# Three modulation rows summed over the partitions by adding transfers instead of by ones-matmuls

## The chip, the cores and the metric

The kernel runs on one core of one Trainium2 chip. The metric is the device time of one execution in microseconds (us); the time before is the median of three runs. Beside them stands one profiled execution of the same kernel, from which all rows below are taken; its times are counted from the start of its span.

## The reference, cut to what matters

One layer of a diffusion backbone on 1024 latent tokens of width 1024 with 256 context tokens. What matters here is the modulation: six rows of 1024 numbers made of the condition `c`, of which three (the shift and scale ahead of the MLP, and the gate behind the mixing sub-layer) are worked out early and used late.

```python
mod_x = (jax.nn.silu(c) @ w_mod[l] + b_mod[l])[:, None, :]
sh1, sc1, gt1, sh2, sc2, gt2 = jnp.split(mod_x, N_MOD, axis=-1)
h_x = _modulate(x, g_pre_mix[l], sh1, sc1)
u_x, q_x, k_x, v_x = _project(h_x, w_in[l])
attn_x = _neighbourhood_attention(q_x, k_x, v_x, k_c, v_c, rpb[l])
mix_x = jnp.concatenate([_pool_mixer(u_x, ...), attn_x], axis=-1) @ w_out[l]
x = x + gt1 * _rmsnorm(mix_x, g_post_mix[l])
y_x = _sq_relu_mlp(_modulate(x, g_pre_mlp[l], sh2, sc2), w_mlp_in[l], w_mlp_out[l])
x = x + gt2 * _rmsnorm(y_x, g_post_mlp[l])
```

## The kernel before

The program is one long line of matmuls on TensorE (PE); the other engines prepare operands and carry results away. Around the change the line is: the key and query products (a Strassen-like scheme of seven products per side, `half_product`, in steps 0 to 23), then 32 attention units `i = (j, m)`, four head pairs `j` by eight token tiles `m`, about 3 us each. Two query products that are left over (`last_query`) fill PE in units 0 and 1. Within the stretch that interests here the order on every engine is the order in which the code is written (`in_order` ties each instruction to the one before it on its engine), so an instruction that waits holds up all that is written behind it on that engine. SyncE (SP) issues the plain transfers; transfers that add (`add_to`) are issued by GpSimd (POOL).

The three rows. `mod_begin` clears a page of 128 x 1024 in SBUF (`accsh`, `accsc`, `acca` for shift, scale and gate; the bias goes into row 0), and `mod_add` adds a 128-row block of the weight times a column of the condition on VectorE (DVE), eight times. Each page then holds 128 partial sums, which are still to be summed over the partitions. The shift's page is stored to DRAM at once (`kept_row`, `row` in the profile) and given back; the other two stay in SBUF.

In units 0 to 6 the sums are finished. `mod_sums_of` multiplies a page by a matrix of ones (four matmuls of 256 columns, so that quarter c of the row stands on partitions 32c to 32c+31); for the gate VectorE multiplies that by `gain`, the norm's gain `gp1` loaded by four broadcasting transfers; for scale and shift ScalarE (ACT) copies it back (`column_sums`). `mod_out` stores the four quarters to DRAM by four transfers of POOL for each row (`ga`, `gsc`, `gsh`). They are read again much later: `columns_of` at units 10 and 12, `gate_page` at unit 30.

What stands beside this work on POOL's queue: `tables(0)`, the bias tables `tab` of the first heads, made of `msk` and `U0w`; `query_parts` and `key_parts` (a cast and a difference each, `qP`, `kP2l`); four adding transfers `y<-y`; and in each unit the copy of the softmax's reciprocal sums, `rb<-ri` (`share`). PE's `turn(i)` in unit i + 2 begins with a transpose of `rb` (line 1312 `pa<-ident,rb`), then transposes the probabilities (`T<-ident,sp`); ACT takes them away (`fifth_kept`, `px`; `turn_kept`, `pt`) and goes on with the exponentials of the unit (`exps`, line 1290); `values` (line 1346) multiplies `pt` by the values. `scores` (line 1259) needs the split keys and queries (`kP0h`, `kP0l`, `qP`), and `biased` on VectorE (line 1279) needs the table.

Near the end of the kernel a fourth row, `accb`, is already summed in the other way: `rows_folded` adds the lower half of the rows to the upper half by one adding transfer, seven times (64, 32, ..., 1 rows). Its lines are

```python
def add_to(to, more):
    nc.gpsimd.dma_start(to, more, accum_op=add)

def rows_folded(rows, *counts):
    for n in counts:
        add_to(rows[:n], rows[n : 2 * n])
```

Of the kernel before, what the change touches and what calls it, by code (L numbers as in the profile page):

```python
# [11 lines left out]
F32 = mybir.dt.float32  # L12
# [6 lines left out]
P = 128  # L19
D = 1024  # L20
# [88 lines left out]
def hybrid_block(ctx, tc, x, ctx_in, w_mod, mod_pages, w_u, b_mod, gp1, gp2, w_in, pool_w, rpb, w_out, w1, w2, vectors,  # L109
                 mask, edge, out):  # L110
    nc = tc.nc
    sub, mul, add = ALU.subtract, ALU.mult, ALU.add
# [6 lines left out]
    dram = ctx.enter_context(tc.tile_pool(name="dram", bufs=1, space=DRAM))  # L119

    def cst(name, shape, dt=F32):
        return const.tile(shape, dt, tag=name, name=name)
# [4 lines left out]
    def page(name, dt=F32):  # L127
        return act.tile([P, 1024], dt, tag="pg", name=name)
# [23 lines left out]
    ones = cst("ones", [P, P])  # L152
# [65 lines left out]
# [3 lines that stand above are left out]
# [40 lines left out]
            mod_add(acc, mod_part(name, c, k), sT, k)  # L261
            yield acc


    def mod_sums_of(name, acc, bank):
        ps = bank(f"pg{name}")
        for c in range(4):
            nc.tensor.matmul(ps[32 * c : 32 * c + 32, :256], ones[:, :32], acc[:, c * 256 : (c + 1) * 256],
                             start=True, stop=True)
        return ps[:, :256]  # L270

    def mod_gain(gp, g, queue):
        quarters = gp.rearrange("(c o f) -> c o f", c=4, o=1)
        for c in range(4):
            queue.dma_start(g[32 * c : 32 * c + 32, :], quarters[c].to_broadcast([32, 256]))
        return g

    def mod_gate(name, acc, g, bank):
        nc.vector.tensor_tensor(acc[:, :256], mod_sums_of(name, acc, bank), g, mul)


    def mod_out(name, acc):
        gates[name] = dram.tile([1, D], F32, tag=f"g{name}", name=f"g{name}")
        for c in range(4):
            nc.gpsimd.dma_start(gates[name][:, c * 256 : (c + 1) * 256], acc[32 * c : 32 * c + 1, :256])

    gates = {}

# [14 lines left out]
    with tc.tile_pool(name="ps1", bufs=6, space=PSUM) as ps1, tc.tile_pool(name="tmp1", bufs=3) as tmp:  # L303

        def bank(name):
            if name[:2] == "pm" or name in ("pxt5", "pxb2", "pxb3", "pxb4", "pxb5", "pcs", "pcr"):
                return lasting(name)
            return ps1.tile([P, 512], F32, tag="mm", name=name)
# [526 lines left out]
        accs = {}  # L835


        kept_row = dram.tile([P, D], F32, tag="row", name="row")

        def mod_parts(name, c, n):  # L840
            accs[name] = mod_begin(name, c, page)
# [4 lines left out]
                    nc.gpsimd.dma_start(kept_row, accs[name])  # L846
                yield


        def column_sums(name, acc, bank):  # L850
            nc.scalar.copy(acc[:, :256], mod_sums_of(name, acc, bank))

        def columns_of(name, to):
            nc.gpsimd.dma_start(to, gates[name].rearrange("o (k p) -> p (o k)", p=P))
# [116 lines left out]
        with tc.issue_after(last[ET.DVE]), tc.issue_after(last[ET.Activation]):  # L971
            for i in range(2):
                ps = bank(f"pvc{i}")
# [49 lines left out]
        rows = [("sc", 4, k) for k in range(4, KT)] + [("a", 2, k) for k in range(KT)]  # L1023
# [22 lines left out]
        def use(step):  # L1046
            for _, put, i in islice(uses, len(plan[step + 1]) if step + 1 < len(plan) else 0):
                put(i)
                fetch()
# [9 lines left out]
        for n, m in enumerate((4, 5, 6, 7, 0, 1, 2, 3)):  # L1059
            ps = bank(f"pv{m}")  # L1060
# [123 lines left out]
        with in_order(ET.PE, ET.Pool, ET.Activation, ET.DVE, ET.SP) as pooling:  # L1184
            banks = {of: [bank(f"p{of}{j}") for j in range(2)] for of in "KQ"}
            use(-1)
            for step, (n, of, j) in enumerate([(n, of, j) for n, of in products for j in range(2)]):
                half_product(n, of, j, banks[of])
                use(step)
                if step in (5, 9, 17):  # L1190
                    name = {5: "S1", 9: "S4", 17: "S3"}[step]
                    parts = token_operand(name, sraw[name])
                if step in (5, 7, 9, 11, 17, 19):
                    next(parts)
                    next(parts)
                if step in (7, 11):
                    name = {7: "S4", 11: "S3"}[step]
                    sraw[name] = token_raw(name)
                if step == 14:
                    mask_page()  # L1200
                if step == 20:
                    for _ in tables(0):
                        pass
                if step in (21, 22):
                    for g in range(2):
                        pool_mixed(2 * (step - 21) + g)
                kept_product(n, of, j, banks[of][j])
                if step == 10:
                    kcs += [page(f"kc{n}", F32R) for n in "hl"]
                    split(kcp, *kcs)  # L1210
                if step == 22:
                    key_parts(0, 0, True)
# [17 lines left out]
    with (  # L1230
# [4 lines left out]
        bank = lasting  # L1235
# [3 lines left out]
        pa, pz = (ps_o.tile([P, 512], F32, tag=n, name=n) for n in ("pa", "pz"))  # L1239
# [208 lines left out]
        with in_order(ET.PE, ET.Activation, ET.DVE, ET.SP) as projected:  # L1448
# [16 lines left out]
            def right_added(j):  # L1465
# [2 lines left out]

            table = [None] + [tables(j) for j in (1, 2, 3)]
            built = lambda j: next(table[j])  # L1470
            out_of = lambda n: mod_out(n, accs[n])
            jobs = {0: [(built, 1), (key_parts, 1, 0), (key_parts, 1, 1)], 1: [(built, 1)], 2: [(built, 1)], 3: [(built, 1)],
                    4: [(built, 1)], 5: [(out_of, "a"), (out_of, "sc")], 6: [(out_of, "sh")], 7: [(query_parts, 1, 1, True, True)],
                    8: [(mixed_split, 0, True)], 9: [(built, 2)],
                    10: [(columns_of, "sc", scale2), (built, 2)], 12: [(columns_of, "sh", s2), (built, 2)],
                    13: [(built, 2), (built, 2)], 14: [(query_parts, 3, 0, False, True)],
# [2 lines left out]
                    21: [(built, 3), (built, 3)], 22: [(key_parts, 3, 1, False, True)], 24: [(mixed_split, 2, True)],  # L1479
                    25: [(query_parts, 3, 1, False, True)], 26: [(weight_split, 0, True)], 28: [(weight_split, 1, True)],  # L1480
                    29: [(weight_split, 2, True)], 30: [(weight_split, 3, True)]}
            rest_of_bank = lambda name: pz[:, 256:]
            for i in range(N):
                if i in LOADS:
                    weight_load(0, kks[LOADS.index(i)])
                if i == N - 2:
                    G1 = gate_page("a")
                if i > 3:
                    weighed(i - 4)
                if i == 0:  # L1490
                    gain = mod_gain(gp1, att.tile([P, 256], F32, tag="gp", name="gpa"), nc.sync)
                    accs["sh"] = page("accsh2")
                    nc.sync.dma_start(accs["sh"], kept_row)
                if i == 2:
                    mod_gate("a", accs["a"], gain, rest_of_bank)
                if i in (5, 6):
                    for k in (2 * i - 10, 2 * i - 9):
                        nc.sync.dma_start(sa2[k], s3[k])
                low()
                scores(i)  # L1500
                biased(i, 0)
                if i < N - 1:
                    biased(i, 1)
                if 8 < i and i % 8 == 3:
                    right_added(i // 8 - 1)
                if 8 < i and i % 8 == 7:
                    add_to(heads[i // 8 - 1][:, :512], sa2[i // 8 - 1])
                for f, *args in jobs.get(i, ()):
                    f(*args)
                if block_copies and (i < 4 or 6 < i):  # L1510
                    block_copied()
                for _ in range(SUMS.count(i)):
                    block_summed()
                if i == 2:
                    late_query = part_page("qP0_1", False)
                    qparts[0, 1] = late_query[:, :512], late_query[:, 512:]
                    high_part(qT[0][1], qparts[0, 1][0])
                if i > 1:
                    turn(i - 2)
                    fifth_kept(i - 2)  # L1520
                if i == 2:
                    turn_kept(0, 0, nc.scalar.copy)
                    column_sums("sc", accs["sc"], lambda name: pa[:, :256])
                if i == N - 1:
                    turn_kept(i - 2, 0, nc.scalar.copy)
                    turn_kept(i - 2, 1, nc.vector.tensor_copy)
                    biased(i, 1)
                exps(i, 0)
                if i == 2:
                    column_sums("sh", accs["sh"], rest_of_bank)  # L1530
                if 2 < i < N - 1:
                    turn_kept(i - 2, 0, nc.scalar.copy)
                exps(i, 1)
                if i == 0:
                    key_parts(2, 0, True, "lo")
                    key_parts(2, 1, True, "lo")
                    query_parts(2, 0, False, "lo")
                if 1 < i < N - 1:
                    turn_kept(i - 2, 1, nc.vector.tensor_copy)
                if i == 2:  # L1540
                    low_part(qT[0][1], *qparts[0, 1])
                for filler in fillers.get(i, ()):
                    last_query(*filler)
                if i > 2:
                    values(i - 3)
# [80 lines left out]
    with tc.tile_pool(name="ps2", bufs=6, space=PSUM) as ps2:  # L1626
# [6 lines left out]
      with ExitStack() as tmp2:  # L1633
# [28 lines left out]
        rows, root = {}, {}  # L1662
# [29 lines left out]
        with tc.issue_after(projected[ET.DVE]), tc.issue_after(projected[ET.Activation]), in_order(ET.Activation, ET.DVE, ET.Pool) as added:  # L1692
# [21 lines left out]
            c = {}  # L1714
# [574 lines left out]
        with tc.issue_after(first[ET.PE]), in_order(ET.PE, ET.Activation, ET.DVE, ET.SP, ET.Pool):  # L2289
# [29 lines left out]
            rows, halves_of_rows = {}, {}  # L2319
# [89 lines left out]
            for name, g in items[: items.index(("P6", 0))]:  # L2409
                if name[0] == "M":  # L2410
                    inner_group(name, g)
                elif name == "P1":
                    if g == 1:
                        gain = page("gpb")[:1]
# [124 lines left out]
```

## Time and profile before

| what | value |
|---|---|
| time, median of 3 runs | 1009.63 us (1009.33 to 1010.6) |
| the profiled execution: its own time | 1009.41 us |
| the profiled execution: span | 1007.6 us |
| PE busy in the span | 997.7 us (99%) |
| DVE, ACT, POOL busy | 799.9, 580.9, 208.8 us |
| ones-matmuls of the three rows (line 268): twelve in the code, 24 on PE | 223.3 to 226.5 us |
| POOL's twelve stores of the rows (line 285) | 235.5 to 242.2 us |

A busy share is an average over the whole run, so it is read with the stretch in mind: the change acts between 157 us, when the scale's page is complete, and 245 us. Rows of the timeline give start, duration, engine, line, operation, output and inputs, and in brackets how long the engine had been idle and what ended that. The chain of waits is followed back from the last instruction; PE stands in it almost all of the time, so time moves when PE is kept waiting or has work taken away.

### The profile page before, as it was taken

What the parts mean: (1) busy time and instruction counts of PE and PEld (TensorE: products, weight loads), DVE (VectorE), ACT (ScalarE), POOL (GpSimd) and SP (SyncE); (2) the same over time, 40 slices, a digit from 0 to 9 for tenths busy, and PEclk for the clock granted to TensorE, in tenths of its full rate; (3) what the DMA queues carried; (4) which work ended last, traced back from release to release, by engine and by line L of the source; (5) the groups of instructions that cost most, each with busy time, mean ns of one, the idle gap of its engine ahead of it and who ended that gap; (6) DMA issues with size and microseconds to landing.
All of it is one profiled execution on the core that took longest, in us unless ns stands there. A gap on an engine that the chain in (4) does not pass through costs nothing.

```text
span 1007.6 us, 16671 instructions
## 1 busy us (share of the span) xinstructions
PE 997.7 (99%) x6054; PEld 829.5 (82%) x6054; DVE 799.9 (79%) x1275; ACT 580.9 (58%) x1038; POOL 208.8 (21%) x280
## 2 busy tenths in 40 slices
PE   8999999999999999999999999999999999999997
PEld 5788888879998888888888888888888888888886
DVE  5589766968885689879998888754798888888895
ACT  6673254448886746786555544544656555545551
POOL 4111110167985232410000000101001000022121
PEclk9999999999999999999999999999999999999999
DMA  9999798665999979986776666724999999579944
GB/s 362 394 284 338 238 275 311 211 158 195 225 189 249 233 195 277 294 209 205 261 253 215 201 212 227 230 93 175 317 369 303 308 340 325 170 219 313 319 166 162
DMA packets 146977, 252.49 MB, mean 251 GB/s; under 512 B 10450, under 2 KB 76882, under 8 KB 146896
## 3 DMA queue, kind: packets, MB, share of 16 engines
q1 hardware_dynamic: 111024, 181.63, 52.7%
q0 software_dynamic: 18736, 38.85, 20.1%
q10 hardware_dynamic: 17136, 30.97, 8.3%
q8 instruction: 47, 0.77, 0.3%
q14 instruction: 34, 0.28, 0.1%
HBM read 197.39 MB, written 69.22 MB: 265 GB/s over the span
## 4 chain that ended last, share of the span: by engine, by line
PE 96%; DVE 1%; DMA 1%; ACT 1%; POOL 0%; issue 0%; SPq 0%; DVEq 0%; POOLq 0%; ACTq 0%
PE pu L485 5%; PE pyiM L2400 4%; PE pyiN L2400 4%; PE pa L1346 4%; PE S L1259 3%; PE phx L230 3%; PE phz L230 3%; PE phv L230 3%; PE pyx L231 3%; PE phz L231 3%; PE phv L231 3%; PE phx L232 3%; PE pyx L230 3%; PE pyx L232 3%; PE phx L231 3%; PE phz L232 3%
## 5 line engine op out<-in xcount | busy, mean ns | idle before, releaser
L1966 ACT ACTIVATE c<-c 128x512 f32<-128x512 f32 x48 | 30.3, 631 | 45.3 <-DVE c L2088 26.6
L174 ACT CAST wpS<-S 128x512 fp32r<-128x512 f32 x64 | 38.7, 617 | 28.7 <-PE phv L232 10.1
L1290 ACT ACTIVATE sp<-sp,nm 128x640 f32<-128x640 f32 (+1 forms) x64 | 51.4, 803 | 6.1 <-DVE ri L1294 5.0
L1279 DVE CUSTOM_DVE_ANT_0 sp<-S,tab 128x640 f32<-128x640 f32 (+1 forms) x56 | 44.5, 795 | 13.0 <-PE pz L1312 10.8
L230 PE MATMUL phx<-thB,wpA 128*128 128x512 f32 x128 | 50.2, 392 | 0.0
L180 DVE TENSOR_TENSOR wpS<-S,wpS 128x512 fp32r<-128x512 f32 x64 | 43.4, 686 | 8.2 <-ACT wpS L174 8.2
L232 PE MATMUL phx<-thB,wpA 128*128 128x512 f32 x128 | 49.8, 389 | 0.0
L231 PE MATMUL phx<-tlB,wpA 128*128 128x512 f32 x128 | 49.8, 389 | 0.0
L216 POOL DMA_DIRECT2D t<-in_w x16 | 19.3, 1207 | 131.4 <-DVE b_0l L180 59.1
L1967 ACT ACTIVATE c<-c 128x512 f32<-128x512 f32 x48 | 30.3, 630 | 15.1 <-DVE sa L2051 12.1
L247 POOL MEMSET accb<- 128x1024 f32 x1 | 1.0, 959 | 142.1 <-ACT c L1967 142.1
L230 PEld LDWEIGHTS phx<-thB,wpA 128*128 128x128 f32 x128 | 24.0, 188 | 5.5 <-ACT s L2019 0.4
L232 PEld LDWEIGHTS phx<-thB,wpA 128*128 128x128 f32 x128 | 24.0, 188 | 5.0
L231 PEld LDWEIGHTS phx<-tlB,wpA 128*128 128x128 f32 x128 | 24.0, 188 | 4.9
L1346 PE MATMUL pa<-pt,v 128*64 128x128 f32 x352 | 25.8, 279 | 0.0
L230 PE MATMUL phz<-thB,wpS 128*128 128x512 f32 x64 | 25.0, 391 | 0.0
L230 PE MATMUL phv<-thT,wpA 128*128 128x512 f32 x64 | 25.0, 391 | 0.0
L231 PE MATMUL phz<-tlB,wpS 128*128 128x512 f32 x64 | 24.9, 390 | 0.0
L231 PE MATMUL phv<-tlT,wpA 128*128 128x512 f32 x64 | 24.9, 389 | 0.0
L232 PE MATMUL phz<-thB,wpS 128*128 128x512 f32 x64 | 24.9, 389 | 0.0
L230 PE MATMUL phy<-thT,wpS 128*128 128x512 f32 x64 | 24.9, 389 | 0.0
L231 PE MATMUL phy<-tlT,wpS 128*128 128x512 f32 x64 | 24.9, 389 | 0.0
(1190 smaller groups left out, 3578.1 us busy)
## 6 DMA issues: line engine op xcount, KB each, us to landing
hrA<-hdA SPq DMA_DIRECT2D x24, 512.0 KB, 7.4
wm<-in_mod_pages SPq DMA_DIRECT2D x16, 512.0 KB, 9.3
wa_0w<-in_w SPq DMA_DIRECT2D x16, 512.0 KB, 4.8
wa_1w<-in_w SPq DMA_DIRECT2D x16, 512.0 KB, 4.3
hdA<-c ACTq DMA_DIRECT2D x32, 256.0 KB, 2.2
hdS<-sa ACTq DMA_DIRECT2D x32, 256.0 KB, 2.6
hqS<-sb ACTq DMA_DIRECT2D x32, 256.0 KB, 3.7
b<-in_w SPq DMA_DIRECT2D x16, 512.0 KB, 8.9
```

The costliest lines, as they stand in the source:

```text
L174: nc.scalar.copy(hi, src)
L180: nc.vector.tensor_tensor(lo, src, hi.bitcast(F32), sub)
L230: nc.tensor.matmul(ps, ahi, bhi, start=first, stop=False, skip_group_check=more)
L231: nc.tensor.matmul(ps, ahi, blo, start=False, stop=False, skip_group_check=more)
L232: nc.tensor.matmul(ps, alo, bhi, start=False, stop=last, skip_group_check=more)
L485: nc.tensor.matmul(pus[b][j], wk(wgt, k, low, j * P, P), r, start=(k == 0 and n == 0), stop=(k == KT - 1 and n == 2))
L1279: nc.vector.tensor_tensor_reduce(out=to, in0=s, in1=bt, scale=1.0, scalar=BIG, op0=add, op1=ALU.min, accum_out=nm)
L1290: nc.scalar.activation(sp, sp, AF.Exp, bias=least[i, e], scale=-1.0, accum_out=sums[i][:, e : e + 1])
L1346: nc.tensor.matmul(pa[e * HD : (e + 1) * HD, cols], v[:, f : f + HD], turns[i][:, e, c] if c < 4 else fifths[i][:, :, (e + 1) * HD : (e + ...
L1966: nc.scalar.activation(r, src, AF.Relu)
L1967: nc.scalar.activation(r, r, AF.Square)
L2400: nc.tensor.matmul(to, a[part][:, j * 256 + t * P : j * 256 + (t + 1) * P], r, start=h + j == 0 and n < 2, stop=ends and n > 1)
```

## The change

The ones-matmuls, the copies back, the twelve stores and the broadcast loads of the gain go. Instead all three pages are folded row by row with `rows_folded`: in each of the product steps 17 to 23 the code now issues three adding transfers, for `accsc` (SBUF), `kept_row` (in DRAM, whose rows are now 256 numbers further apart) and `accs["a"]` (SBUF), of 64, 32, 16, 8, 4, 2 and 1 rows. Row 0 then holds the sum. In unit 0 SP stores the scale's row to `gsc` and loads the gain as one row; in unit 1 VectorE multiplies the gate's one row by it (`gate_kept`) and SP stores it to `ga`. The shift's row is read where it lies.

```diff
-    def mod_sums_of(name, acc, bank):
-        ps = bank(f"pg{name}")
-        for c in range(4):
-            nc.tensor.matmul(ps[32 * c : 32 * c + 32, :256], ones[:, :32], acc[:, c * 256 : (c + 1) * 256],
-                             start=True, stop=True)
-        return ps[:, :256]
...
-    def mod_gate(name, acc, g, bank):
-        nc.vector.tensor_tensor(acc[:, :256], mod_sums_of(name, acc, bank), g, mul)
-
-    def mod_out(name, acc):
-        gates[name] = dram.tile([1, D], F32, tag=f"g{name}", name=f"g{name}")
-        for c in range(4):
-            nc.gpsimd.dma_start(gates[name][:, c * 256 : (c + 1) * 256], acc[32 * c : 32 * c + 1, :256])
...
-        kept_row = dram.tile([P, D], F32, tag="row", name="row")
+        kept_row = dram.tile([P, D + 256], F32, tag="row", name="row")[:, :D]
...
-        def column_sums(name, acc, bank):
-            nc.scalar.copy(acc[:, :256], mod_sums_of(name, acc, bank))
...
                 half_product(n, of, j, banks[of])
                 use(step)
+                if step > 16:
+                    for rows in (accs["sc"], kept_row, accs["a"]):
+                        rows_folded(rows, 64 >> step - 17)
...
                 if step == 20:
                     for _ in tables(0):
                         pass
...
-            out_of = lambda n: mod_out(n, accs[n])
+            def gate_kept():
+                nc.vector.tensor_tensor(accs["a"][:1], accs["a"][:1], gain, mul)
+                gates["a"] = dram.tile([1, D], F32, tag="ga", name="ga")
+                nc.sync.dma_start(gates["a"], accs["a"][:1])
-            jobs = {0: [...], 1: [(built, 1)], ...
-                    4: [(built, 1)], 5: [(out_of, "a"), (out_of, "sc")], 6: [(out_of, "sh")], 7: ...
+            jobs = {0: [...], 1: [(built, 1), (gate_kept,)], ...
+                    4: [(built, 1)], 7: ...
...
                 if i == 0:
-                    gain = mod_gain(gp1, att.tile([P, 256], F32, tag="gp", name="gpa"), nc.sync)
-                    accs["sh"] = page("accsh2")
-                    nc.sync.dma_start(accs["sh"], kept_row)
-                if i == 2:
-                    mod_gate("a", accs["a"], gain, rest_of_bank)
+                    gain = page("gpa")[:1]
+                    nc.sync.dma_start(gain, gp1.rearrange("(o d) -> o d", o=1))
+                    gates["sh"], gates["sc"] = kept_row[:1], dram.tile([1, D], F32, tag="gsc", name="gsc")
+                    nc.sync.dma_start(gates["sc"], accs["sc"][:1])
...
                 if i == 2:
                     turn_kept(0, 0, nc.scalar.copy)
-                    column_sums("sc", accs["sc"], lambda name: pa[:, :256])
...
                 exps(i, 0)
-                if i == 2:
-                    column_sums("sh", accs["sh"], rest_of_bank)
```

Where this puts the instructions. First POOL's queue behind the clearing of the gate's page. Before, the tables come next, then the split of the second head pair's query (`qP`) and the four `y` adds:

```order
L248 DMA acca<-in_b_mod 1x16x64
L1100 MEMSET tab_1993 128x256
L1100 MEMSET tab_1994 128x256
L1113 TENSOR_TENSOR tab_1993<-msk,U0w 128x128 x6
L1113 TENSOR_TENSOR tab_1994<-msk,U0w 128x128 x6
L1126 CAST qP_0_2102<-q_0_1705 128x512
L1127 TENSOR_TENSOR qP_0_2102<-q_0_1705,qP_0_2102 128x512
L216 DMA y_1366<-y_1366 128x512
L216 DMA y_1416<-y_1416 128x512
L216 DMA y_1456<-y_1456 128x512
L216 DMA y_1525<-y_1525 128x512
```

Now twelve folds stand ahead of the tables and nine behind them; each fold of a page waits for the landing of the fold before it of the same page. The piece shows the fourth round, the tables and the first half of what follows (the rounds of 64, 32 and 16 rows stand ahead of it, one more round and then `qP` behind it):

```order
L216 DMA accsc<-accsc 8x1024
L216 DMA row<-row 8x1024
L216 DMA acca<-acca 8x1024
L1075 MEMSET tab_2005 128x256
L1075 MEMSET tab_2006 128x256
L1088 TENSOR_TENSOR tab_2005<-msk,U0w 128x128 x6
L1088 TENSOR_TENSOR tab_2006<-msk,U0w 128x128 x6
L216 DMA accsc<-accsc 4x1024
L216 DMA row<-row 4x1024
L216 DMA acca<-acca 4x1024
L216 DMA accsc<-accsc 2x1024
L216 DMA row<-row 2x1024
```

What moved: the tables stand behind twelve folds, and `qP`, the `y` adds, `kP2l` and the first `rb` copy behind all twenty-one.

On PE the ones-matmuls of the gate (x4 at line 268) stood between the last query product and the scores of unit 2:

```order
L230 MATMUL pqv_2096<-hx_7_701,wQT4h 128x512
L231 MATMUL pqv_2096<-hx_7_701,wQT4h 128x512
L232 MATMUL pqv_2096<-hx_7_701,wQT4l 128x512
L268 MATMUL pz<-acca,ones 32x256 x4
L1259 MATMUL S_2_0_2254<-kP0h,qP_0_2097 128x384
L1259 MATMUL S_2_1_2255<-kP0h,qP_0_2097 128x384
L1259 MATMUL S_2_0_2254<-kP0l,qP_0_2097 128x384
```

and now the scores follow the product directly (`S_2_0` and `S_2_1` are the two heads' scores of that unit):

```order
L230 MATMUL pqv_2117<-hx_7_701,wQT4h 128x512
L231 MATMUL pqv_2117<-hx_7_701,wQT4h 128x512
L232 MATMUL pqv_2117<-hx_7_701,wQT4l 128x512
L1237 MATMUL S_2_0_2270<-kP0h,qP_0_2118 128x384
L1237 MATMUL S_2_1_2271<-kP0h,qP_0_2118 128x384
L1237 MATMUL S_2_0_2270<-kP0l,qP_0_2118 128x384
```

What moved: four matmuls are gone here, and in the same way the eight of scale and shift behind the transposes of unit 2; nothing else on PE changes place.

On SP, around the loads for the tables (`U0w` for the first heads, `U_...` for the second; `t3q` is a copy of MLP weights that is needed much later), it was

```order
L1093 DMA msk<-in_mask 128x768
L1105 DMA U0w<-in_rpb 128x1x489 x2
L275 DMA gpa<-in_gp 32x256 x4
L1493 DMA accsh_2131<-row 128x1024
L1105 DMA U_2157<-in_rpb 128x1x489 x2
L1365 DMA t3q_2079<-in_w 128x2x512 x4
L1498 DMA ss_2093<-y_1366 128x512
```

and now is

```order
L1068 DMA msk<-in_mask 128x768
L1080 DMA U0w<-in_rpb 128x1x489 x2
L1474 DMA gpa<-in_gp 1x1024
L1476 DMA gsc<-accsc 1x1024
L1080 DMA U_2175<-in_rpb 128x1x489 x2
L1343 DMA t3q_2100<-in_w 128x2x512
L1453 DMA ga<-acca 1x1024
L1343 DMA t3q_2100<-in_w 128x2x512 x3
L1479 DMA ss_2114<-y_1366 128x512
```

What moved: the store of the scale's row, which waits for that page's last fold, stands ahead of the second heads' table load, and the store of the gate's row, which waits for VectorE's product, among the `t3q` copies. On DVE the product `acca<-acca,gpa` of 1 x 1024 stands behind the bias of unit 1 and ahead of the two sums `q<-pqv` of the last query product; before, the gate's 128 x 256 product stood behind those two.

More of the change, by code (lines that the diff above doesn't have):

```diff
@@ L262, in mod_sum @@
             yield acc
-    def mod_sums_of(name, acc, bank):
-        ps = bank(f"pg{name}")
-        for c in range(4):
-            nc.tensor.matmul(ps[32 * c : 32 * c + 32, :256], ones[:, :32], acc[:, c * 256 : (c + 1) * 256],
-                             start=True, stop=True)
-        return ps[:, :256]
-    def mod_gain(gp, g, queue):
-        quarters = gp.rearrange("(c o f) -> c o f", c=4, o=1)
-        for c in range(4):
-            queue.dma_start(g[32 * c : 32 * c + 32, :], quarters[c].to_broadcast([32, 256]))
-        return g
-    def mod_gate(name, acc, g, bank):
-        nc.vector.tensor_tensor(acc[:, :256], mod_sums_of(name, acc, bank), g, mul)
-    def mod_out(name, acc):
-        gates[name] = dram.tile([1, D], F32, tag=f"g{name}", name=f"g{name}")
-        for c in range(4):
-            nc.gpsimd.dma_start(gates[name][:, c * 256 : (c + 1) * 256], acc[32 * c : 32 * c + 1, :256])
     gates = {}
@@ L1470, in hybrid_block @@
             built = lambda j: next(table[j])
-            out_of = lambda n: mod_out(n, accs[n])
-            jobs = {0: [(built, 1), (key_parts, 1, 0), (key_parts, 1, 1)], 1: [(built, 1)], 2: [(built, 1)], 3: [(built, 1)],
-                    4: [(built, 1)], 5: [(out_of, "a"), (out_of, "sc")], 6: [(out_of, "sh")], 7: [(query_parts, 1, 1, True, True)],
+            def gate_kept():
+                nc.vector.tensor_tensor(accs["a"][:1], accs["a"][:1], gain, mul)
+                gates["a"] = dram.tile([1, D], F32, tag="ga", name="ga")
+                nc.sync.dma_start(gates["a"], accs["a"][:1])
+            jobs = {0: [(built, 1), (key_parts, 1, 0), (key_parts, 1, 1)], 1: [(built, 1), (gate_kept,)], 2: [(built, 1)], 3: [(built, 1)],
+                    4: [(built, 1)], 7: [(query_parts, 1, 1, True, True)],
                     8: [(mixed_split, 0, True)], 9: [(built, 2)],
@@ L1481, in hybrid_block @@
                     29: [(weight_split, 2, True)], 30: [(weight_split, 3, True)]}
-            rest_of_bank = lambda name: pz[:, 256:]
             for i in range(N):
```

## The prediction

> **What bounds the kernel now.** I read the page first, then the chain of waits, then the timelines of PE and POOL around the change.
>
> ```profile
> PE 997.7 (99%) x6054; PEld 829.5 (82%) x6054; DVE 799.9 (79%) x1275; ACT 580.9 (58%) x1038; POOL 208.8 (21%) x280
> ...
> PE 96%; DVE 1%; DMA 1%; ACT 1%; POOL 0%; issue 0%; SPq 0%; DVEq 0%; POOLq 0%; ACTq 0%
> ```
>
> TensorE is busy for 99% of the span and is 96% of the chain. So only two things move time: matmuls taken away, and waits that PE did not have. The chain through units 2 to 7 shows which waits end last there (start, duration, what):
>
> ```profile
> 225.54 0.61 PE pa L268 x8
> ...
> 226.44 0.92 ACT sp L1290 x2
> 227.37 0.26 ACT accsh L851
> 227.63 0.82 ACT sp L1290 x2
> ...
> 228.71 1.09 PE pa L1346 x16
> ...
> 239.47 0.31 POOL rb L1296
> ...
> 239.82 0.27 PE pa L1312
> ```
>
> Behind the ones-matmuls of line 268 the chain goes over ScalarE's exponentials, between which the copy `accsh` stands, to `values` at 228.71, and at 239.47 it passes POOL's copy `rb`. PE's own rows of that place:
>
> ```profile
> 223.27 0.64 PE L268 MATMUL pz<-acca,ones 128*32 128x256 f32 x8
> ...
> 224.82 0.21 PE L1312 MATMUL pa<-ident,rb 64*128 64x64 f32 x1
> ...
> 225.47 0.64 PE L268 MATMUL pa<-accsc,ones 128*32 128x256 f32 x8
> ...
> 226.47 0.68 PE L1259 MATMUL S<-kP0h,qP 64*128 64x384 f32 x2
> ...
> 239.82 0.14 PEld L1312 LDWEIGHTS pa<-ident,rb 64*128 64x128 f32 x1 [0.31 <-POOL rb L1296]
> ```
>
> The reader is to see 224.82: there PE needs the first `rb`. Whether it gets it depends on POOL, whose queue the change fills:
>
> ```profile
> 197.78 0.31 POOL L1100 MEMSET tab<- 128x256 f32 x1 [58.07 <-PE pQ L232]
> ...
> 198.74 6.85 POOL L1113 TENSOR_TENSOR tab<-msk,U0w 128x128 f32<-128x128 f32 x12
> 210.03 0.62 POOL L1126 CAST qP<-q 128x512 fp32r<-128x512 f32 x1 [4.44 <-PE pK L232]
> 210.72 1.71 POOL L1127 TENSOR_TENSOR qP<-q,qP 128x512 fp32r<-128x512 f32 x1
> 212.37 3.55 POOL L216 DMA_DIRECT2D y<-y  x4
> 214.60 1.89 POOL L1100 MEMSET tab<- 128x256 f32 x2
> 218.37 2.55 POOL L1127 TENSOR_TENSOR kP2l<-kT,kP2h 128x512 fp32r<-128x512 f32 x2 [1.88 <-ACT kP2h L1126]
> 220.89 1.28 POOL L1127 TENSOR_TENSOR qP<-q,qP 128x512 fp32r<-128x512 f32 x1
> 222.12 0.28 POOL L1296 COPY rb<-ri 128x128 f32<-128x128 f32 x1
> ```
>
> POOL is idle for 58 us up to 197.78, but from there to the end of `rb` at 222.40 its gaps come to only 4.4 and 1.9 us, and `rb` is 2.4 us early. That is all the room the folds have once they run past 197.8.
>
> **What is taken away.** The gate's ones-matmuls are 0.57 us of PE (223.27 to the scores), those of scale and shift 1.0 us (225.47 to 226.47). Behind the latter PE waits for ScalarE anyway: `values` goes at 228.71 when the exponentials are through, so there only the two copies count, 0.26 us for `accsh` and, I take it, as much for `accsc`: 0.5. The twelve stores made `rb` late at 239.8, 0.31 us. If nothing else waited, the gain would be 0.57 + 0.5 + 0.31 = 1.4 us, at most 1.9 with the full 1.0. Both lie under 0.2% of the run (2.0 us), which is about what a measurement of this kernel can tell from no change. The gain's loads, the page reload and the gate's 128x256 product lie beside PE and cost nothing now.
>
> **What is added: the folds.** Each waits for the one before it of its page, on POOL's queue, with everything behind it. The trace has such a chain near its end, `accb` (64 to 1 rows), and its last landing:
>
> ```profile
> 629.08 0.82 POOL L216 DMA_DIRECT2D accb<-accb  x1 [46.10 <-DVE accb L255]
> 634.95 0.79 POOL L216 DMA_DIRECT2D accb<-accb  x1 [5.05 <-DMA accb<-accb]
> 641.13 0.77 POOL L216 DMA_DIRECT2D accb<-accb  x1 [5.39 <-DMA accb<-accb]
> 644.28 0.82 POOL L216 DMA_DIRECT2D accb<-accb  x1 [2.39 <-DMA accb<-accb]
> 647.77 0.80 POOL L216 DMA_DIRECT2D accb<-accb  x1 [2.67 <-DMA accb<-accb]
> 652.29 0.79 POOL L216 DMA_DIRECT2D accb<-accb  x1 [3.72 <-DMA accb<-accb]
> 657.57 0.78 POOL L216 DMA_DIRECT2D accb<-accb  x1 [4.49 <-DMA accb<-accb]
> ...
> accb<-accb POOLq DMA_DIRECT2D x1, 4.0 KB, 2.0
> ```
>
> From one fold to the next it takes R = 5.87, 6.18, 3.15, 3.49, 4.52 and 5.28 us. It follows the load of the DMA engines, not the size. In windows of time (DMA share and GB/s stand last):
>
> ```profile
> 192.00:194.00 2.00, 2.00 (x11) 1.65 (x10) 2.00 (x4) 1.16 (x3) 0.00 (x0) 1.00 0.99 331
> ...
> 198.00:202.00 4.00, 4.00 (x19) 3.33 (x18) 2.81 (x4) 2.10 (x3) 3.63 (x8) 1.00 0.19 49
> ...
> 632.00:635.00 3.00, 3.00 (x15) 2.48 (x14) 2.31 (x4) 1.26 (x3) 0.05 (x1) 1.00 1.05 255
> ...
> 641.00:644.30 3.30, 3.30 (x17) 2.71 (x16) 1.61 (x3) 1.62 (x3) 0.78 (x2) 1.00 0.25 43
> ```
>
> At a share of 1.05 R is 5.87, at 0.25 it is 3.15. When the chain starts:
>
> ```profile
> 189.24 1.28 DVE L255 SCALAR_TENSOR_TENSOR acca<-wma_7w,sx,acca 128x1024 f32<-128x1024 f32 x1
> ...
> 627.49 1.29 DVE L255 SCALAR_TENSOR_TENSOR accb<-wmb_7w,sx,accb 128x1024 f32<-128x1024 f32 x1 [1.19 <-DMA wmb_7w<-in_w_mod]
> ...
> y<-y POOLq DMA_DIRECT2D x2, 256.0 KB, 4.1
> ...
> 205.62 1.16 ACT L176 ACTIVATE mix<-y 128x512 fp32r<-128x512 f32 x2 [4.63 <-POOL tab L1113]
> ...
> 220.66 0.69 DVE L1176 TENSOR_TENSOR q<-pqv,q 128x512 f32<-128x512 f32 x1 [1.23 <-PE pqv L232]
> ```
>
> The scale's and shift's first folds go long before, while POOL is idle. But the third of the first round, the gate's, needs the page that VectorE completes at 190.52, and all later rounds stand behind it. `accb` started 0.3 us after its product, so this one starts at 190.8. The sum:
> - R of 64 rows: the DMA share is 0.99 then, so 5.9 as for `accb` (bound below: 4.1 + 0.3 = 4.4, the landing of a `y` add of the same 256 KB).
> - R of 32 and of 16 rows: the queues are nearly empty (0.19). Below, a round can't be shorter than its three issues, 3 x 0.78 = 2.35, and a landing of 2.0 plus 0.3 gives the same; above, 6.18 at full load. I take 2.9, nearer the 3.15 measured at 0.25.
> - The gate's fold of 8 rows: 0.8. Start at 190.8 + 5.9 + 2.9 + 2.9 = 202.5, done 203.3.
> - Tables: two clears of 0.31 and 6.85: 203.3 + 7.5 = 210.8, where they were done at 205.6.
> - Second block: two R of 2.9 and three last issues, 2.35: 8.15, to 218.9.
> - The same work as before to `rb`: 2.34 (210.03 to 212.37), 3.55, 0.57 to the end of the clears at 216.49, and 4.03 (218.37 to 222.40): 10.5, to 229.4.
>
> In short `rb` ends at 211.95 + the sum of five R, here 17.5. PE's transposes start at 229.4 instead of 224.82, 4.6 us later; the gate's 0.57 of matmuls vanishes in that wait. Behind it 0.5 and 0.31 are won. Net +3.8: 1009.41 + 3.8 = **1013.2 us**. The 1009.41 is the profiled execution's own time, 0.2 below the median of the runs; its span is 1.8 shorter, and I leave that difference as it is.
>
> [...]
>
> **Smaller parts.** The tables, late by 5.2, also hold up ScalarE's `mix` (its wait for POOL's `tab` is in the row at 205.62) and with it the keys `kP0h` for unit 0, so some of PE's wait, up to 2 us, will stand at the first scores instead; `rb` is then later still, so the sum stays. VectorE's product of one row waits for the gate's last landing (about 218.2 + 2.0 = 220.2), and costs at most the 1.28 of a full page; behind it wait the two `q<-pqv`, which had 1.2 us to spare, and their reader, the second half of the first query. All this ends ahead of 229. On SP the scale's store waits for its last fold (about 218.5), and the second table load behind it goes some 4 us late; it must have landed when POOL has made `rb`. The 1.5 MB of folds use queues that stand idle.
>
> **The rivals.**
> 1. Not slower: the rounds run at the floor, 2.35, and the first at 4.4. Five R are then 13.8, `rb` ends at 225.75, 0.9 late, and the 0.8 behind it pays for that: 1009.5; with less still, 1008.0 (all 1.4 won). It decides at a sum of 13.6 for the five R. For it: the empty queues at 198. Against it: no `accb` step but the last landing was that short.
> 2. The folds behave as `accb` did throughout: 5.87 + 6.18 + 3.15 + 4.52 + 5.28 = 25.0, `rb` at 237, 12.1 late, less 0.8: 1020.7. Against it: its steps met loads that aren't here.
> 3. SP's late table load holds POOL behind `rb`, so that the second `rb` is late: about 2 us on top, 1015.2. Against it: `rb` itself is late by more.
> 4. PE resumes slowly after its wait: the windows above have the clock at 1.00 and PE busy throughout, so no row shows it. If work of half the net wait's 3.8 us then took double time, 1.9 us would be added: 1015.1. [...]
>
> **How the numbers follow.** Forecast 0.50 (own range 1010.6 to 1016), rival 1 0.26 (1007.6 to 1011), rival 2 0.10, rivals 3 and 4 0.07 each. Slower by over 0.2% takes most of the forecast and rivals 2 to 4: 0.68. Within 0.2%: most of rival 1 and the forecast's low end: 0.26. Faster: 0.06, since even the whole 1.9 is short of 0.2%. The range 1008.2 to 1018.5 leaves out the best of rival 1 and most of rival 2.
>
> **What would show it.** In the profile after: the tables on POOL near 203 to 211 (before 198.7 to 205.6), the first `rb` near 229, a wait of PE's line 1312 `pa<-ident,rb` for POOL `rb` of 2 to 5 us, none at the later units, and no line 268. Wrong if the gate's folds follow each other in under 2.5 us, or if POOL issues later folds while earlier ones are under way.

## The result: 1021.9 us, 12 us slower

The changed kernel takes 1021.88 us (median of five runs, 1019.33 to 1022.99) against 1009.63 before (1009.33 to 1010.6): a ratio of 1.0116 (of the means, as in every run below), 95% interval 1.0100 to 1.0133. The forecast was 1013.2 with a range to 1018.5: the sign was right, the size a third of what came. The profiled execution took 1020.96 us, its span 1019.2, 11.6 more than before. The page of the changed kernel, engines and shares of the chain:

```profile
PE 1002.3 (98%) x6030; PEld 833.3 (82%) x6030; DVE 803.6 (79%) x1275; ACT 580.0 (57%) x1036; POOL 216.5 (21%) x289
...
PE 93%; DVE 3%; ACT 1%; issue 1%; DMA 1%; POOL 1%; SPq 0%; ACTq 0%; DVEq 0%; POOLq 0%
```

PE has 24 instructions less, yet is busy 4.6 us longer, and its share of the chain has fallen by three points. What PE waited for between 120 and 280 us, where it waited for nothing before (engine, line, releaser; us in total, times, longest):

```profile
PE S L1237 <- DVE kT L1151: 4.1, 1, 4.1
PE T L1290 <- DVE q L1151: 1.7, 2, 1.5
PE pa L1290 <- POOL rb L1274: 1.0, 1, 1.0
```

There are two places: ahead of the first scores (line 1237), and at the first transposes (line 1290); in the kernel before these are lines 1259 and 1312. The same stretch in windows. Behind the length of each stand PE's busy time (and instructions), the clock granted to PE as a share of full speed, the busy share of the DMA engines, and GB/s.

```profile
213.00:217.40 4.40, 0.34 (x4) 0.96 0.10 11
217.40:219.00 1.60, 1.60 (x12) 0.50 0.10 15
219.00:221.00 2.00, 2.00 (x7) 0.50 0.08 8
221.00:223.00 2.00, 2.00 (x6) 0.50 0.06 3
223.00:225.00 2.00, 2.00 (x14) 0.78 0.26 49
225.00:227.00 2.00, 2.00 (x15) 1.00 1.00 192
...
231.00:233.00 2.00, 1.11 (x13) 1.00 1.11 201
233.00:235.00 2.00, 0.43 (x3) 0.78 0.63 115
235.00:237.00 2.00, 1.72 (x19) 0.50 0.57 145
237.00:239.00 2.00, 2.00 (x22) 0.50 1.05 282
239.00:241.00 2.00, 2.00 (x27) 0.51 0.96 259
241.00:243.00 2.00, 2.00 (x41) 1.00 1.06 401
```

Behind each place the granted clock was 0.50 for over 6 us. That is why PE is busy longer with less work. What the clock cost is estimated as busy time times (1 - clock): 0.80 + 1.00 + 1.00 + 0.44 = 3.2 us behind the first wait, and 0.09 + 0.86 + 1.00 + 0.98 = 2.9 behind the second. The whole difference, in PE's order:

| | us |
|---|---|
| PE already later at the last product, 0.4 of it a longer wait at the start (`pxt`, 1.4 for 1.0) | +0.6 |
| wait ahead of the first scores | +4.1 |
| half clock behind it | +3.2 |
| wait for `rb` at the first transposes | +1.0 |
| waits for the late query behind it, 1.50 and 0.17 | +1.7 |
| half clock behind those | +2.9 |
| ones-matmuls gone (0.57 and 1.0), wait behind the twelve stores gone (0.31) | -1.9 |
| sum; measured 11.6 | 11.6 |

The half-clock terms are good to a few tenths: by the start times in PE's two timelines the scores of unit 0 are 4.77 us late and those of unit 1 7.73, so the first half clock cost 3.0 and not 3.2.

Who made PE wait is in POOL's queue:

```profile
193.44 0.82 POOL L216 DMA_DIRECT2D acca<-acca  x1 [33.53 <-DVE acca L255]
...
201.30 0.77 POOL L216 DMA_DIRECT2D acca<-acca  x1 [5.44 <-DMA acca<-acca]
...
204.75 0.76 POOL L216 DMA_DIRECT2D acca<-acca  x1 [0.93 <-DMA acca<-acca]
...
207.85 0.79 POOL L216 DMA_DIRECT2D acca<-acca  x1 [0.56 <-DMA acca<-acca]
...
208.90 5.14 POOL L1088 TENSOR_TENSOR tab<-msk,U0w 128x128 f32<-128x128 f32 x12
...
214.86 1.60 POOL L216 DMA_DIRECT2D acca<-acca  x1
...
218.62 0.84 POOL L216 DMA_DIRECT2D acca<-acca  x1
...
221.64 1.37 POOL L216 DMA_DIRECT2D acca<-acca  x1
...
227.70 3.86 POOL L1102 TENSOR_TENSOR kP2l<-kT,kP2h 128x512 fp32r<-128x512 f32 x2
230.20 2.58 POOL L1102 TENSOR_TENSOR qP<-q,qP 128x512 fp32r<-128x512 f32 x1
231.43 1.58 POOL L1274 COPY rb<-ri 128x128 f32<-128x128 f32 x1
```

The tables end at 214.0 (before 205.6) and the first `rb` at 233.0 (before 222.4). ScalarE's and VectorE's rows there:

```profile
214.08 0.63 ACT L176 ACTIVATE mix<-y 128x512 fp32r<-128x512 f32 x1 [10.77 <-POOL tab L1088]
...
191.87 1.27 DVE L255 SCALAR_TENSOR_TENSOR acca<-wma_7w,sx,acca 128x1024 f32<-128x1024 f32 x1
...
228.22 5.87 DVE L1451 TENSOR_TENSOR acca<-acca,gpa 1x1024 f32<-1x1024 f32 x1
234.03 1.27 DVE L1151 TENSOR_TENSOR q<-pqv,q 128x512 f32<-128x512 f32 x2
```

`mix`, held by the tables for 10.77 us, leads over VectorE's sums to the keys of unit 0: the first wait. And the gate's product of one row took 5.87 us; behind it stood the two last query sums, which the first transposes needed: the second.

### The profile page after: what moved, and what is told of

The parts are those of the page before. It is cut to its first block, busy times and chain, and to the rows that moved or that the text cites. A ratio compares the mean times of both kernels' runs of the same rounds, so it can differ in the third digit from the quotient of the medians.

```text
span 1019.2 us, 16627 instructions
## 1 busy us (share of the span) xinstructions
PE 1002.3 (98%) x6030; PEld 833.3 (82%) x6030; DVE 803.6 (79%) x1275; ACT 580.0 (57%) x1036; POOL 216.5 (21%) x289
## 4 chain that ended last, share of the span: by engine, by line
PE 93%; DVE 3%; ACT 1%; issue 1%; DMA 1%; POOL 1%; SPq 0%; ACTq 0%; DVEq 0%; POOLq 0%
PE pu L463 4%; PE pyiM L2378 4%; PE pyiN L2378 4%; PE pa L1324 4%; PE S L1237 3%; PE phx L230 3%; PE phz L230 3%; PE phz L232 3%; PE phx L231 3%; PE phx L232 3%; PE phz L231 3%; PE pyx L231 3%; PE phv L230 3%; PE pyx L232 3%; PE phv L232 3%; PE phv L231 3%
## 5 line engine op out<-in xcount | busy, mean ns | idle before, releaser
L230 PE MATMUL phv<-thT,wpA 128*128 128x512 f32 x64 | 25.0, 391 | 0.0
L232 PE MATMUL phv<-thT,wpA 128*128 128x512 f32 x64 | 24.9, 389 | 0.0
```

The lines of the kernel that those rows point to most:

```text
L230: nc.tensor.matmul(ps, ahi, bhi, start=first, stop=False, skip_group_check=more)
L232: nc.tensor.matmul(ps, alo, bhi, start=False, stop=last, skip_group_check=more)
```

## The experiments

Theory: three things cost. The gate's chain of folds ahead of the tables makes the first wait; a wait brings half clock; VectorE's product, held by POOL's work beside it, makes the second wait. Rivals: the clock falls with the transfers; one row is slow as such; the three chains crowd each other.

**The wait and the clock, without any fold.** In the kernel before, POOL writes some pieces of the first tables again (same values), so that the tables end later. 21 more pieces, 12 more, and 7 more:

```diff
-                    for i in range(3):
+                    for i in [0] * (EXTRA[e][a] if j == 0 else 0) + [0, 1, 2]:
```

> The kernel before with 21 more of POOL's table pieces (the same values written again, 0.41 us each), so that the first tables end 8.6 us later, near 214.2 as in the changed kernel, and no fold anywhere. Theory: PE waits some 4.1 us ahead of the first scores and then runs at half clock for 6 us: 4.1 + 3.0 = 7.1 more, about 1016.7. Rival: the clock fell with the folds' transfers and not with the wait: 4.1 more, 1013.7, clock at 1.00.

> As the kernel with 21 more table pieces, with 12 more: the tables end 4.9 us later, near 210.5, and PE's wait ahead of the first scores is 1.0 to 1.5 us. If the half clock needs a wait of several us, it doesn't come: about 1.3 more, 1010.9. If any wait that the profile shows brings it: 1.3 + 3.0, 1013.9.

> The kernel before with 7 more of POOL's table pieces (12 made the tables end at 213.6 and PE wait 4.9 us, 0.67 us each): the tables end near 210.3, and PE waits 1.3 to 1.9 us ahead of the first scores. Theory: the half clock comes only with a longer idle time, so the wait is all: 1.6 more than before, about 1010.6, clock at 1.00. Rival: any such wait brings 6.6 us of half clock: 1.6 + 3.2, 1013.8.

A piece took 0.55 to 0.6 us (6.85 for twelve in the kernel before) and not 0.41, so the first two came later than meant; the waits in the profiled executions were 8.52, 4.88 and 0.96 us. The times are 1020.83 (ratio 1.0117, 1.0104 to 1.0131), 1016.14 (1.0076, 1.0062 to 1.0090) and 1011.50 us (1.0023, 1.0014 to 1.0032): 11.9, 7.2 and 2.4 more than the kernel before beside them, always more than the wait. (The profiled execution with 12 pieces took 1018.41, 2.3 more than the median, so its wait is not the median's.) PE's wait with 12 more pieces, and its windows, as above:

```profile
PE S L1261 <- DVE kT L1178: 4.9, 1, 4.9
```

```profile
217.00:219.00 2.00, 0.92 (x8) 0.64 1.06 177
219.00:221.00 2.00, 2.00 (x11) 0.50 1.10 185
221.00:223.00 2.00, 2.00 (x6) 0.50 0.99 177
```

The half clock is there with no fold in the program. With 7 more pieces the profiled execution had none, and nine of the eleven runs lie between 1010.3 and 1012.1 at a mean clock of 0.998 to 1.000; the two others took 1013.75 and 1014.84 at 0.996 and 0.995, about 3 us more; they have no profile. So a wait of a microsecond or so probably brings the half clock now and then, one of 4 us and more did in every profile here.

Last the counter-test: 12 more pieces, and 20 matmuls on PE in the wait, written where a later product starts anew.

```diff
             last_query("P7", 0)
+            for k in range(20):
+                nc.tensor.matmul(last_queries[1], weights["T3", "Q"][0][:, :P], rows_of["S3"][k % 4][0], start=True, stop=True)
```

> The kernel before with 12 more table pieces (PE waited 4.9 us ahead of the first scores there, then ran 6.8 us at half clock; 1016.1), and 20 more matmuls of 128x512 on PE in that wait, 0.227 us each, 4.5 in all, whose results are overwritten. Theory: the half clock follows from PE standing still, so it doesn't come: PE waits 0.4 us, the clock stays at 1.00, and only the lateness is left, 4.9 us: 1014. Rival: the clock falls for another reason (the late tables' work on POOL and VectorE, or scores of another shape); then 1016 to 1018 as without the filling.

```profile
217.00:219.00 2.00, 2.00 (x16) 1.00 1.11 190
219.00:221.00 2.00, 2.00 (x12) 1.00 1.13 174
```

1014.28 us (1.0049, 1.0035 to 1.0063): 1.9 less than with PE idle, 5.2 over the kernel before, which is the lateness and little else. The two intervals just touch; it is the clock, 1.00 with the same late tables and nearly the same DMA share, that decides. It follows from PE's standing still, and the theory holds.

**The gate's product.** Moved from unit 1 to unit 6, alone:

```diff
-   1: [(built, 1), (gate_kept,)], ... 4: [(built, 1)], 7:
+   1: [(built, 1)], ... 4: [(built, 1)], 6: [(gate_kept,)], 7:
```

> The changed kernel with one edit: the gate's one-row product and its store stand in unit 6 and not in unit 1. Theory: in the changed kernel the product held VectorE for 5.87 us ahead of the two last query sums, and PE's waits of 0.96 (rb), 1.50 and 0.28 us there were followed by 6 us at a granted clock of 0.50. Without it the waits of 1.50 and 0.28 go, the one for rb stays, PE comes back at full speed, and the time falls by 1.8 + 3.0 to about 1016; the first wait (4.1 us ahead of the first scores) stays. The product itself takes about 1.2 us in its new place. Rival A: POOL's late rb alone sets the second wait; the time stays at 1020 to 1022. Rival B: the product is slow because it has one row; then it takes 5.9 us in unit 6 too, and PE waits there.

```profile
247.65 1.21 DVE L1451 TENSOR_TENSOR acca<-acca,gpa 1x1024 f32<-1x1024 f32 x1
```

```profile
PE S L1237 <- DVE kT L1151: 4.4, 1, 4.4
PE pa L1290 <- POOL rb L1274: 1.4, 1, 1.4
PE pK L230 <- DVE kT L1143: 1.0, 1, 1.0
PE pa L1324 <- ACT px L1304: 0.9, 1, 0.9
PE pa L1290 <- DVE f L1334: 0.9, 1, 0.9
```

The one row takes 1.21 us there, the waits of 1.50 and 0.17 us and the second half clock are gone. But the time, 1019.35 us (1.0100, 1.0087 to 1.0114), fell by 2.5 and not by 4.8; against the kernel before beside each it is 10.4 for 12.2, and the intervals of the two ratios overlap, so the gain is read from the profile and not from the time. In its place the product made PE wait 0.9 in unit 6 (last row), and this execution had 1.0 us at a product ahead of the gate's folds and 0.9 at the first `values` (line 1324) that the changed kernel's didn't. Done on all 128 rows, in the old place:

```diff
-                nc.vector.tensor_tensor(accs["a"][:1], accs["a"][:1], gain, mul)
+                nc.vector.tensor_tensor(accs["a"], accs["a"], gain, mul)
```

> The changed kernel with the gate's product done on all 128 rows (the gain is loaded 128 times), in the same place; the 127 other rows are not used. Theory: VectorE's product has two operands in SBUF and stands still while POOL's splits of 128x512 run beside it, so its place and not its width makes it long: 5 to 6 us again, time 1020 to 1023. Rival: one row is slow as such; then it takes 1.3 us as the pages of 128x1024 do, the second wait shrinks to rb's 1 us, and the time is about 1016.

```profile
228.09 4.44 DVE L1451 TENSOR_TENSOR acca<-acca,gpa 128x1024 f32<-128x1024 f32 x1
```

4.44 us and 1021.11 us (1.0123, 1.0108 to 1.0139), so it is the place and not the row. (This profiled execution, 1017.30 us, is the fastest of the four, and has no second half clock; the others took 1020.73 to 1022.64.) And with POOL's three splits of unit 0 given to ScalarE and VectorE:

```diff
-                    key_parts(2, 0, True, "lo")
-                    key_parts(2, 1, True, "lo")
-                    query_parts(2, 0, False, "lo")
+                    key_parts(2, 0, True)
+                    key_parts(2, 1, True)
+                    query_parts(2, 0, False)
```

> The changed kernel with the splits of the third head pair's keys and first query (3 x 1.25 us of POOL in unit 0, beside the gate's product) done by ScalarE and VectorE, so that POOL runs none of them beside the product. Read for the product's own duration. Theory: POOL's reads of SBUF held it; now it takes 1.2 to 1.7 us (the table pieces and rb still run there). Rival: something else of the place (its transfers, its operands just landed) held it: 3 to 6 us as before.

```profile
230.63 2.16 DVE L1451 TENSOR_TENSOR acca<-acca,gpa 1x1024 f32<-1x1024 f32 x1
```

2.16 us, more than the 1.2 to 1.7 expected and well under 5.87 (one run, 1017.63 us): by this one profile, POOL's splits are the larger part of what held it; the rest wasn't separated (`rb` and table pieces remained beside it).

**Which folds.** Scale's and shift's moved ahead to steps 10 to 16, the gate's alone in steps 17 to 23:

```diff
-                if step > 16:
-                    for rows in (accs["sc"], kept_row, accs["a"]):
-                        rows_folded(rows, 64 >> step - 17)
+                if 9 < step < 17:
+                    for kept in (accs["sc"], kept_row):
+                        rows_folded(kept, 64 >> step - 10)
+                if step > 16:
+                    rows_folded(accs["a"], 64 >> step - 17)
```

> The changed kernel with scale's and shift's folds moved ahead, so that in steps 17 to 23 the gate's seven folds stand alone, with the tables and unit 0 behind them as in the changed kernel; the product stays in unit 1. Theory: the gate's own chain sets the rounds, since POOL stands still for each landing: tables end at 211 to 214, PE waits 1.5 to 4 us at the first scores with 6.6 us of half clock behind, rb and the product are late again; 1017 to 1021. Rival: three chains at once made the rounds long; then they run at 2 to 2.5 us, the tables end near 207, no wait at the first scores, and the time is 1010 to 1013.

```profile
164.28 0.79 POOL L216 DMA_DIRECT2D accsc<-accsc  x1 [5.01 <-DMA accsc<-accsc]
...
171.57 0.78 POOL L216 DMA_DIRECT2D accsc<-accsc  x1 [3.96 <-DMA accsc<-accsc]
...
178.26 0.81 POOL L216 DMA_DIRECT2D accsc<-accsc  x1 [4.48 <-DMA accsc<-accsc]
...
194.37 1.11 POOL L216 DMA_DIRECT2D acca<-acca  x1
201.75 0.78 POOL L216 DMA_DIRECT2D acca<-acca  x1 [6.27 <-DMA acca<-acca]
205.18 0.77 POOL L216 DMA_DIRECT2D acca<-acca  x1 [2.65 <-DMA acca<-acca]
208.32 0.80 POOL L216 DMA_DIRECT2D acca<-acca  x1 [2.36 <-DMA acca<-acca]
```

Alone, the gate's rounds are 7.38, 3.43 and 3.14 us, as with the others beside (7.86, 3.45, 3.10), and the tables are as late (7.38 + 3.43 + 3.14 from 194.37, and then the tables): crowding falls. The upper rows are scale's folds of 32, 16 and 8 rows: the rounds of 32 and 16 took 7.29 and 6.69 us, in a stretch (150 to 200) at a DMA share of 0.93, where the gate's of the same sizes took 3.43 and 3.14 at 0.38 and 0.20. So among folds of one size the load of the DMA engines made a round long or short. The time, 1017.27 us (1.0084, 1.0071 to 1.0098), is 4.6 under the changed kernel (8.1 for 12.2 over the kernel before beside each) with one issue behind the tables in each round and not three, a product of 3.12 us, and no second half clock in the profile.

The other way round, the gate's folds moved into units 3, 6, 8, 10, 12, 14 and 16, its product to unit 19; and in a second kernel the row also goes through DRAM into columns, so that the product is 128x8:

```diff
-                    for rows in (accs["sc"], kept_row, accs["a"]):
+                    for rows in (accs["sc"], kept_row):
...
+                if i in FOLDS:
+                    rows_folded(accs["a"], 64 >> FOLDS.index(i))
... in the second:
+                nc.vector.tensor_tensor(gatec, gatec, gain, mul)
+                nc.sync.dma_start(gates["a"].rearrange("o (k p) -> p (o k)", p=P), gatec)
```

> The changed kernel with only the gate's seven folds moved: scale and shift stay in the product steps, the gate's are issued in units 3, 6, 8, 10, 12, 14 and 16 (6 to 9 us apart, each landed before the next), the product of one row and its store in unit 19. Theory: the waits are the gate folds' alone. The tables end near 205.6 again, PE waits nowhere at the first scores or rb, the clock stays at 1.00, the 1.4 to 1.9 us of removed ones-matmuls and stores show, less 0.9 for the product in a unit (as it cost in unit 6): 0.5 to 1.0 below the kernel before, about 1008.2. Rival: the folds of scale and shift hold POOL as well; the tables stay late and the time above 1014.

> As the kernel with the gate's folds spread, and the gate's folded row goes through DRAM into 8 columns of 128 rows, is multiplied there by the gain's columns (128x8 in place of 1x1024) in unit 27, and is stored back as a row. Theory: the product costs about 0.1 us and nobody waits for it, so all of the 1.4 to 1.9 us shows: about 1007.4. Rival: the 4-byte transfers of the columns hold POOL or SP in the units; then no better than the kernel with the row product.

Of the first, PE's waits between 120 and 320 us:

```profile
PE pa L1290 <- POOL rb L1274: 3.5, 4, 1.9
PE pa L1290 <- DVE f L1334: 3.1, 2, 2.8
```

The wait at the first scores is gone, as the theory says, and its half clock with it. Yet the time is 1019.60 us (1.0100, 1.0086 to 1.0114): I took POOL to have room in the units. A row of the kernel before, which I had not weighed, says otherwise (POOL's busy time is the fifth behind the window's length):

```profile
260.00:300.00 40.00, 40.00 (x722) 36.41 (x718) 32.83 (x97) 35.45 (x98) 36.66 (x60) 1.00 1.02 212
```

36.66 of 40 us are taken there, so an issue of 0.8 us makes `rb` later: three of the four waits for it, 1.9, 0.3 and 0.5, stand there (the fourth, 0.8, is the first `rb`, behind the folds of scale and shift that stayed). The 2.8 for `f` is the product's. The gate's last fold was issued at 274.25, and the product stands behind its landing; over 260 to 300 the mean granted clock was 0.96, which is some 3 us at 0.50. The one in columns is worse still, 1024.75 (1.0157, 1.0143 to 1.0171). Its profile has a wait of 3.8 us at one `pa` that it puts down to "issue", near the 4-byte stores, with a mean granted clock of 0.98 over 300 to 400, and one of 2.5 at a `poz`; whether the stores made them was not tried.

Two more tries at a better version. Only scale and shift folded, ahead of the tables, with the gate as before (an edit of the kernel before):

```diff
+                if 9 < step < 17:
+                    for kept in (accs["sc"], kept_row):
+                        rows_folded(kept, 64 >> step - 10)
...
-                    column_sums("sc", accs["sc"], lambda name: pa[:, :256])
...
-                    column_sums("sh", accs["sh"], rest_of_bank)
```

> The kernel before with only scale and shift folded, in steps 10 to 16, where POOL has nothing else to do until the tables; the gate stays with its ones-matmuls, its product and its four stores. Theory: none of the folds that POOL waits for stands ahead of work that PE needs, so no wait comes, and the 1.0 us of ones-matmuls for scale and shift and the 0.3 of PE's wait behind eight stores go: 1.0 to 1.3 below the kernel before, less up to 0.7 us where the folds of 64 rows make a weight late near 180 (as in the run with the gate's folds spread): about 1008.2, at the edge of what can be told. Rival: any fold ahead of unit 0 costs; 1011 or more.

```profile
PE pK L230 <- DVE kT L1165: 0.7, 1, 0.7
```

1011.95 us (1.0033, 1.0021 to 1.0046): slower than before by 2.9. No `rb` is late; what PE waits for are 0.7 us near 180 for a key sum (the row) and 0.7 at scores of unit 3, about what was won. That the folds delay the loads behind the first of these is likely, but not tested: the changed kernel issues the same two 64-row folds there, and its profile has no such wait. Nor can the 2.9 be read from this profile, which is of the fastest of the five executions (1010.77); the rest of it isn't accounted for. And the gate's folds in POOL's gaps: 64 rows behind the tables, 32 behind the `y` adds, the rest in units 1 to 5, the product in four pieces:

```diff
                     for _ in tables(0):
                         pass
+                    rows_folded(accs["a"], 64)
...
                     add_to(s3[k], s1a[k])
+                rows_folded(accs["a"], 32)
...
+                if 0 < i < 6:
+                    rows_folded(accs["a"], 32 >> i)
+                if i in (6, 11, 15, 19):
+                    gate_kept((6, 11, 15, 19).index(i))
```

> All three folded: scale and shift in steps 10 to 16, the gate's fold of 64 rows right behind the tables, that of 32 behind the y adds, the others in units 1 to 5, each some 3 us behind the last one's issue, and the gate's product in four pieces of 256 in units 6, 11, 15 and 19. Theory: POOL's gaps there (1.4 to 2.7 us of each unit) hold an issue of 0.8 and what is left of a landing of 2.5 to 3.2; PE waits nowhere, or 0.5 us in a unit or two; 1007.5 to 1009. Rival: one fold a unit is too close, each rb comes later and later, and PE waits 0.5 to 1 us in units 1 to 5: 1011 to 1014, as the gate's folds in units 6 to 16 cost.

Of its DMA issues and PE's waits:

```profile
acca<-acca POOLq DMA_DIRECT2D x1, 128.0 KB, 10.4
```

```profile
PE pa L1291 <- DVE f L1335: 2.3, 1, 2.3
PE pK L230 <- DVE kT L1143: 1.8, 1, 1.8
```

1019.45 us (1.0098, 1.0084 to 1.0112). Behind the `y` adds the fold of 32 rows took 10.4 us to land, so the next one held POOL for 2.3 us in unit 1, and the one behind it came late too; PE waited 1.0 for an `rb`. But the larger waits are others: 1.8 near 180 for a key sum, as with scale and shift alone, and 2.3 where VectorE's first piece of the product stands behind the last fold (issued at 243.47; PE went on at 247.21). The clock was at 0.50 for 3.4 us behind the wait for `rb` and again behind the last. No version found beats the kernel before.

## Why the prediction was right and wrong

- **The path was right.** "`rb` ends at 211.95 + the sum of five R": measured R, from the gate's rows, are 7.86, 3.45, 3.10, 3.76 and 3.02, 21.2 in all; 233.1 by the formula, 233.0 in the trace. Two errors in it cancel: VectorE finished the gate's page at 193.1 and not at 190.5, and the fold of 8 rows and the tables took 6.2 us instead of 8.3. Why the page was late wasn't followed up.
- **The sum of the R was too small**, 17.5 for 21.2. Worst was the first, 5.9 for 7.86. I had read R as following the load of the DMA engines and not the size, and the folds of scale and shift ahead bear that out (7.29 us for 32 rows, 6.69 for 16, in a stretch at 0.93); but from one share of 0.99 I took `accb`'s 5.87, and the first round took 7.86 at 0.96 here and 7.38 with the gate alone. The four others, taken as 2.9 each, were 3.0 to 3.8: the queues were less empty than I took them to be for two of them (shares of 0.57 and 0.45 and not 0.19). The 3.7 that were missing make 1016.9 of 1013.2.
- **The product of one row was the step that failed outright.** "Costs at most the 1.28 of a full page" took the price of an instruction that ran alone. It took 5.87, and "all this ends ahead of 229" was wrong: the query sums came at 234.0 to 235.3. Price: 1.7 us of waits.
- **Rival 4 was true, and I gave it 0.07.** PE resumed at half clock, twice. I priced 1.9 us; it cost 6.1, of which the first 3.2 disappeared in the wait for `rb` that PE would have had anyway, and 2.9 came on top. The term behind the 1.9, work of half the net wait in double time, is shown by no run: what came was 6.8 us at a granted clock of 0.50 in each of the two places.
- From 1016.9, 1.7 and 2.9 more, and 0.5 less if all of scale's and shift's ones-matmuls counted (1.0 for my 0.5; PE had no idle time there, but no run shows this term alone), are 1021.0. The profiled execution took 1020.96.
- **Where the wait stands.** I expected 2 to 5 us at `pa<-ident,rb` and up to 2 at the first scores. It was 4.1 at the scores and 1.0 at `rb`: the tables, 8.4 us late and not 5.2, stopped PE first. That the folds wait for each other was right; that POOL issues no later fold of a page while the earlier one is under way, too.
- Rival 2 (R as slow as `accb`'s throughout) gave 1020.7, nearly the time, for another reason: the sum of the R was 21.2 and not 25. Rival 1 needed later rounds of 2.35; none was under 3.02. Rival 3 didn't come: POOL's second `rb` waited 0.99 us for VectorE's `ri`, and for no load.

## What to carry over

An accumulating transfer in an in-order queue costs what stands behind it: count every round as a stop of that queue (the gate's rounds took 3.0 to 7.9 us here), and place the chain where the queue has nothing that the bound engine needs. A microsecond of PE's idle time isn't a microsecond: here each wait of 4 us or more had 2 to 3 us of half clock on top, and shorter ones had between nothing and 3. And before an instruction moves beside another engine's, look at what runs there: the product of one row took 5.87 us beside three of POOL's splits, 2.16 without them and 1.21 in unit 6.

## What the hardware showed beyond what I had expected

- **The half clock comes in blocks.** In windows of 0.4 us the changed kernel was at 0.50 from 217.1 to 223.9 and from 234.1 to 241.0, 6.8 us each. Elsewhere the block was 10.2 us (21 more table pieces) or about 3.4 (in the gaps, twice, by mean clocks of 0.86, 0.72 and 0.57 in windows of 4 us; with the folds spread 3.2, by the 0.96 over 40 us), so the lengths seen are near one, two and three times 3.4. It followed waits of 4.07, 4.88 and 8.52; with the full-width product a wait of 2.45 for `rb` did not bring it (in the one execution profiled), while 2.8 with the folds spread and, in the changed kernel, 0.96 and 1.50 did. So below 4 us the length of a wait didn't decide. Nor did PE have to stand still without a break: in the 3.4 us ahead of the fall at 234.1 it was busy for 1.69 us.
- **VectorE was held through several of POOL's instructions.** The product ended at 234.09, 1.08 us after POOL's splits and `rb` (done at 233.01) had gone by, and in unit 6 it took 1.21; so it seems to have moved only then, though no run shows when it began. It took 5.87 us beside POOL's three splits of unit 0 and 2.16 without them; by the rows above it was held through four of POOL's instructions in a row. That the cause is what the two engines read, as the theories of two of the runs have it, neither shows: the splits went as a whole.
- **A fold's round went by the load and not by its rows**: 7.29 us for 32 rows in a stretch at a DMA share of 0.93, 3.43 for 32 rows at 0.38, both in the kernel with the gate's folds alone. Two things stay open: no fold of 64 rows met empty queues, and one late round in that kernel took 4.45 us at a share of 0.04 (217.45 to 221.90), with a split on POOL beside it.
